# A planned two-layer decoder trunk on one core: the last norms by square root and reciprocal, fifteen weight loads taken from GpSimd, and six new seeds for the order

## The chip, the cores and the metric

The kernel runs on one core of a Trainium2 chip. The metric is the device time of one execution in microseconds (us), the median over several runs. The core has five engines that run side by side, each through its own list of instructions in a fixed order: TensorE (PE in the profile; PEld is its weight load), VectorE (DVE), ScalarE (ACT), GpSimd (POOL) and SyncE (SP, which here only issues transfers). Instructions of different engines wait for each other by semaphores. Transfers between the chip's memory and the on-chip buffers are done by DMA engines; SP issues most of them, GpSimd those that add what they read to what lies in the buffer.

## The reference

Two layers of a decoder over 512 positions and 1024 channels. Layer 0 mixes positions with a gated recurrence (RG-LRU), layer 1 with a chunked gated linear attention (GLA); each mixer is followed by a gated feed-forward net with a convolution of width 3. A condition vector `c` gives shift, scale and gate of each of the four sublayers.

```python
def rmsnorm(x, g):
    y = x32 * lax.rsqrt(jnp.mean(x32 * x32, axis=-1, keepdims=True) + EPS)
    return (y * g.astype(jnp.float32)).astype(x.dtype)

def reference(x, c, ada_w, ...):
    c_act = jax.nn.silu(c)
    for i in range(DEPTH):                                   # DEPTH = 2
        mod = (c_act @ ada_w[i] + ada_b[i])[:, None, :]
        sh_m, sc_m, gt_m, sh_f, sc_f, gt_f = jnp.split(mod, 6, axis=-1)
        h = rmsnorm(x, norm_g[i, 0]) * (1.0 + sc_m) + sh_m
        y = rglru_mixer(h, ...) if i % 2 == 0 else gla_mixer(h, ...)
        x = x + gt_m * rmsnorm(y, norm_g[i, 1])
        h = rmsnorm(x, norm_g[i, 2]) * (1.0 + sc_f) + sh_f
        y = conv_ffn(h, ffn_w_up[i], ffn_conv_w[i], ffn_conv_b[i], ffn_w_down[i])
        x = x + gt_f * rmsnorm(y, norm_g[i, 3])
    return x
```

## The kernel before

All matrix products are done in three passes of a reduced 32-bit format: each operand is split into a rounded part (hi) and a rest (lo), and TensorE sums hi·hi, hi·lo and lo·hi. So every weight that comes from memory (tile `raw`, mostly 128x1024, 512 KB) is prepared into two halves of a tile `w` (or into tiles `g`): ScalarE casts the first half (`CAST w<-raw`), and the second half, raw minus that cast, is made in one of two ways. In the first VectorE subtracts (`TENSOR_TENSOR w<-raw,w`). In the second, taken for the units that the rule `BYLOAD` picks, ScalarE writes the raw values rounded and negated (`ACTIVATE w<-raw`), and GpSimd issues a second transfer of the same 512 KB, which adds the weight from memory to that (`accum`), so that the rest is left. `load_upto` does this for one unit after another; units named `up` are columns of the feed-forward nets' first projection (layer, column), `gr` those of GLA's output gate, `gv` of its values, `rgg` of the recurrence's gate. GpSimd also issues 46 adding transfers that form sums of weight blocks for the down projections (tile `raw`); the change leaves these alone.

The stages in time are the prologue (norm of x, the condition's `adaT` products), RG-LRU, feed-forward 0, GLA (about 530 to 790 us), feed-forward 1 and `last_down` (from about 1085 us).

The order on each engine is not written by hand. The program first lists some thousand operations (`Sched.add`) with an estimated duration; `Sched.order` then simulates the engines and picks, whenever one is free, the ready operation of the highest priority. On TensorE and SP that is the place in the program. On VectorE, ScalarE and GpSimd it is the longest chain of work still behind the operation, plus a random nudge (`NUDGE` 0.5 us times a normal number, drawn from `SEEDS`, one seed for each of six segments of the program). Two limits bind the order to the buffers: `raw` and `araw` have 3 buffers each, `mm` 7 banks, `w` 8, so a transfer can be issued only when its buffer has been read for the last time.

`last_down` ends the kernel. For each of four tiles t of 128 positions TensorE makes 2 x 512 columns of the down projection into banks `mm`; VectorE adds each bank to y; ScalarE squares it and sums the squares (`Square` with an accumulator); `rstd_col` makes the norm's factor: `mean_of` on VectorE, then a power of -1/2 on GpSimd (`TENSOR_TENSOR sm<-sm,const`). VectorE multiplies y by the gate's rows, then adds factor times y to the residual `xo` (`SCALAR_TENSOR_TENSOR g<-const,sm,g`), which SP stores. For the last tile the second half is cut in two 256-wide parts, so that the chain after the last matmul is short, and its last 256 columns are scaled by ScalarE (`z`) and added by GpSimd. Between feed-forward 0 and GLA `gate_rows` writes a gate's 1024 values to memory and reads them back spread over all partitions (`g<-dram`).

Of the kernel before, what the change touches and what calls it, by code (L numbers as in the profile page):

```python
# [8 lines left out]
F32 = mybir.dt.float32  # L9
# [6 lines left out]
P = 128  # L16
# [258 lines left out]
BANK_AHEAD = 1  # L275
BANK_FROM = lambda s: s.mix2
LATE = 0.6, 0.6
SEEDS, NUDGE = (10, 10, 10, 10, 10, 10), 0.5
MARGIN = {"dve": 1.04, "act": 1.04}
RINGS = "araw",  # L280
ENGS = ("pe", "dve", "act", "pool", "sp")
# [364 lines left out]
                   after=after)  # L646


BYLOAD = lambda what, *i: what in ('rgg', 'gv', 'gr') or what == 'up' and (i[0] == 1 and i[1] >= KF and 4 <= i[1] - KF < 18 and i[1] % 2 or i[0] == 0 and i[1] >= KF and 4 <= i[1] - KF)
WARM = (3, 2, 2, 2)  # L650
KSPLIT = 2
NAH = 4
# [12 lines left out]
def trunk(ctx, tc, xT, x_d, wall, adaT, par_d, c_d, walpha_d, ident_d, masks_d, out):  # L665
# [363 lines left out]
    def rstd_col(ss, n):  # L1029
# [2 lines left out]
        e.pow(rp[0:1], mean_of(ss, n), nhalf[0:1])  # L1032
        return rp[0:1]

    xkept = {}

    def sublayer_out(sub, src, y, gate, nexth, held=None, xo=None, old=None):
# [75 lines left out]
    def last_down(hid, y, rows, xo, old):  # L1113

        for t in range(NT):
            old(t)
        for t in range(NT):
            last = t == NT - 1
            groups = [[(0, S)], [(S, S + 256)], [(S + 256, D)]] if last else [[(0, S), (S, D)]]
            ss = s.buf("sm", F32, 4)  # L1120
            yg = []
            i = 0
            for g in groups:
                for ps, (f0, f1) in zip(down_t("f1", hid, t, g), g):
                    yv = y[2 * t + f0 // S][f0 % S:f0 % S + f1 - f0]
                    e.tt(yv, yv, ps, ALU.add)
                    sq = gtn(f1 - f0)
                    e.act(sq, yv, AF.Square, accum=ss[i:i + 1])
                    i += 1
                    yg.append((yv, f0, f1))  # L1130
            rp = rstd_col(ss, i)
            for yv, f0, f1 in yg:
                e.tt(yv, yv, rows[f0 // S][f0 % S:f0 % S + f1 - f0], ALU.mult)
            ys = [y[2 * t + f][:] for f in range(2)]
            if last:

                z = gtn(256)
                e.act(z, ys[1].sub(256, S), AF.Copy, scale=rp)
                xr = xo[t, 1][256:S]
                e.tt(xr, xr, z, ALU.add, "pool")  # L1140
            for f, yv in enumerate(ys):
                for c0, c1 in ((0, 256), (256, S))[:2 - f] if last else ((0, S),):
                    xr = xo[t, f][c0:c1]
                    e.stt(xr, yv.sub(c0, c1), rp, xr, ALU.mult, ALU.add)
                e.store(out[t, :, f * S:(f + 1) * S], xo[t, f][:], P * S * 4)


    def conv3(layer, ps, m):
# [684 lines left out]
```

## Time and profile before

| | |
|---|---|
| runs, us | 1129.80, 1130.26, 1128.26; median 1129.80 |
| the profiled execution's own time | 1129.75 us |
| its span, first to last instruction | 1128.0 us |
| mean granted clock of TensorE | 0.997 |
| busy: TensorE, VectorE, ScalarE, GpSimd | 1105.5, 912.2, 673.9, 113.8 us |
| GpSimd's adding transfers | 95 (49 into `w`, 46 into `raw`) |

A row of the timeline reads: start, duration, engine, line, operation, output<-inputs, shapes, count; in brackets the time that the engine sat idle before it and what released it. A row of groups reads: line, engine, operation, names, shapes, count | busy us, mean ns of one | idle time before and its releasers. A row of windows reads: the stretch, its length, busy us of TensorE, weight load, VectorE, ScalarE, GpSimd with counts, then the granted clock, the DMA engines' busy share and GB/s. Buffer numbers are left out in all of them.

### The profile page before, as it was taken

Reading aid. Unit: us, or ns where it says so; the run is one execution under the profiler, and the core shown is the slowest. Engines: PE = TensorE matmul, PEld = TensorE weight load, DVE = VectorE, ACT = ScalarE, POOL = GpSimd, SP = SyncE. Lnnn points to the kernel's source line nnn. Section 1 sums busy time; section 2 is a strip of 40 time slices with the busy share of each in tenths; the row PEclk is TensorE's granted clock in tenths of the full one; section 3 lists DMA queues with packets and bytes.
Section 4 is the critical chain, followed back from the end, with each engine's and each line's share of the span. In section 5 each row is a group of like instructions: output and inputs, shape, how many; then the busy total and the mean of one; then the engine's idle time right before and its main releaser. Section 6 shows DMA issues by size and latency. Waiting matters only on the chain.

```text
span 1128.0 us, 14808 instructions
## 1 busy us (share of the span) xinstructions
PE 1105.5 (98%) x5293; PEld 919.2 (81%) x5293; DVE 912.2 (81%) x1559; ACT 673.9 (60%) x1039; POOL 113.8 (10%) x144
## 2 busy tenths in 40 slices
PE   7999999999999999999999999999999999999996
PEld 6776889888888888787888888889888888888885
DVE  6998999878878888898779797756876867777897
ACT  4569958656456354466797748656556454553432
POOL 0000011011101101101101101002000100010001
PEclk9999999999999999999999999999999999999998
DMA  9889876699898999873553927227487766767642
GB/s 362 287 249 294 285 235 241 168 260 315 240 267 243 273 269 263 204 221 116 151 141 107 302 78 206 94 100 241 112 257 211 198 188 157 199 158 196 169 130 75
DMA packets 67068, 232.97 MB, mean 207 GB/s; under 512 B 7473, under 2 KB 8145, under 8 KB 66994
## 3 DMA queue, kind: packets, MB, share of 16 engines
q1 hardware_dynamic: 53314, 182.73, 46.2%
q0 software_dynamic: 13680, 49.29, 24.0%
q8 instruction: 42, 0.69, 0.2%
q14 instruction: 32, 0.26, 0.1%
HBM read 225.68 MB, written 6.31 MB: 206 GB/s over the span
## 4 chain that ended last, share of the span: by engine, by line
PE 72%; DMA 14%; DVE 5%; ACT 4%; issue 3%; POOL 0%; SPq 0%; DVEq 0%; POOLq 0%; ACTq 0%
PE mm L621 71%; DMA raw<-in_wall_dram 10%; DMA w<-in_adaT_dram 2%; DVE w L544 1%; ACT g L594 1%; ACT w L601 1%; DMA g<-dram 1%; DVE g L544 1%; DVE g L558 1%; PE mm L628 1%; DMA const<-in_par_dram 1%; DVE const L544 1%; PE nr L621 1%; ACT w L594 0%; DVE const L558 0%
## 5 line engine op out<-in xcount | busy, mean ns | idle before, releaser
L621 PE MATMUL mm<-g,w 128*128 128x512 f32 (+2 forms) x2758 | 613.5, 380 | 1.1 <-DVE g L558 0.7
L621 PEld LDWEIGHTS mm<-g,w 128*128 128x128 f32 (+1 forms) x2758 | 501.0, 187 | 100.6 <-issue 1.4
L621 PE MATMUL mm<-w,g 128*128 128x512 f32 (+1 forms) x1428 | 330.6, 389 | 0.8 <-DVE g L544 0.8
L621 PEld LDWEIGHTS mm<-w,g 128*128 128x128 f32 x1428 | 265.2, 188 | 55.6 <-DVE g L544 1.2
L601 ACT CAST w<-raw 128x1024 fp32r<-128x1024 f32 x206 | 212.3, 1040 | 135.1 <-DMA raw<-in_wall_dram 122.0
L544 DVE TENSOR_TENSOR w<-raw,w 128x1024 fp32r<-128x1024 f32 x157 | 188.0, 1208 | 43.1 <-ACT w L601 42.8
L558 DVE SCALAR_TENSOR_TENSOR g<-mm,const,g 128x510 f32<-128x510 f32 (+3 forms) x199 | 147.9, 747 | 65.7 <-ACT g L594 62.7
L544 DVE TENSOR_TENSOR g<-g,g 128x256 f32<-128x256 f32 (+2 forms) x251 | 135.5, 564 | 32.6 <-ACT g L594 20.3
L594 ACT ACTIVATE g<-mm,const 128x512 f32<-128x512 f32 x115 | 86.6, 761 | 73.9 <-PE mm L621 73.1
L637 POOL DMA_DIRECT2D w<-in_wall_dram x49 | 42.6, 870 | 521.3 <-ACT w L594 417.1
L558 DVE SCALAR_TENSOR_TENSOR araw<-araw,const 128x1024 f32<-128x1024 f32 x72 | 86.7, 1219 | 5.9 <-DMA araw<-in_adaT_dram 5.9
L594 ACT ACTIVATE g<-g 128x512 f32<-128x512 f32 (+1 forms) x136 | 68.9, 541 | 26.1 <-DVE g L558 19.8
L601 ACT CAST g<-g 128x512 fp32r<-128x512 f32 (+2 forms) x84 | 49.9, 605 | 50.7 <-DVE g L544 50.7
L621 PE MATMUL mm<-g,g 128*128 128x256 f32 (+3 forms) x508 | 78.1, 309 | 1.1 <-DVE sm L569 1.1
L621 PEld LDWEIGHTS mm<-g,g 128*128 128x128 f32 (+1 forms) x508 | 70.5, 191 | 6.5 <-DVE g L544 1.3
L594 ACT ACTIVATE w<-raw 128x1024 fp32r<-128x1024 f32 x49 | 51.9, 1059 | 21.6 <-DMA raw<-in_wall_dram 20.0
L637 POOL DMA_DIRECT2D raw<-in_wall_dram x46 | 40.0, 869 | 198.3 <-ACT raw L594 47.2
L544 DVE TENSOR_TENSOR const<-const,mm 128x512 f32<-128x512 f32 (+1 forms) x81 | 53.4, 676 | 7.0 <-PE mm L621 6.6
L549 POOL TENSOR_TENSOR sm<-sm,const 128x1 f32<-128x1 f32 (+1 forms) x30 | 25.5, 854 | 271.5 <-DVE sm L558 237.7
L594 ACT ACTIVATE g<-const 128x512 f32<-128x512 f32 x47 | 29.0, 630 | 33.3 <-DVE const L544 19.6
L594 ACT ACTIVATE g<-mm 128x512 f32<-128x512 f32 x44 | 26.2, 596 | 27.6 <-DVE g L544 14.2
L594 ACT ACT_TABLE_LOAD x28 | 35.9, 1283 | 3.5 <-PE nr L621 2.3
(119 smaller groups left out, 752.8 us busy)
## 6 DMA issues: line engine op xcount, KB each, us to landing
raw<-in_wall_dram SPq DMA_DIRECT2D x218, 512.0 KB, 4.8
araw<-in_adaT_dram SPq DMA_DIRECT2D x72, 512.0 KB, 7.5
w<-in_wall_dram POOLq DMA_DIRECT2D x49, 512.0 KB, 8.4
raw<-in_wall_dram POOLq DMA_DIRECT2D x44, 512.0 KB, 8.1
w<-in_adaT_dram SPq DMA_DIRECT2D x24, 512.0 KB, 8.4
g<-dram SPq DMA_DIRECT2D x24, 256.0 KB, 5.7
dram<-const SPq DMA_DIRECT2D x8, 512.0 KB, 3.0
const<-in_xT_dram SPq DMA_DIRECT2D x4, 512.0 KB, 5.7
```

Source lines behind the costliest of these rows:

```text
L544: self.s.add(eng, dur, lambda: e.tensor_tensor(out.ap(), a.ap(), b.ap(), op=op), [a, b], [out])
L549: lambda: self.nc.gpsimd.tensor_tensor(out.ap(), a.ap(), b.ap(), op=ALU.pow), [a, b], [out])
L558: return self.nc.vector.scalar_tensor_tensor(out.ap(), a.ap(), f(sc), b.ap(), op0=op0, op1=op1, **kw)
L594: return self.nc.scalar.activation(out.ap(), a.ap(), func, **kw)
L601: self.s.add("act", (0.095 if self._sb(a) else 0.052) + out.n * 0.8325e-3, lambda: self.nc.scalar.copy(out.ap(), a.ap()), [a], [out], afte ...
L621: r.append(self.nc.tensor.matmul(g[0].ap(), g[1].ap(), g[2].ap(), start=g[3], stop=g[4], **kw))
L628: self.s.add("pe", 0.112, lambda: self.nc.tensor.transpose(out.ap(), a.ap(), ident.ap()), [a, ident], [out])
L637: self.s.add("pool", 0.9, lambda: self.nc.gpsimd.dma_start(out.ap(), src, accum_op=ALU.add), [out], [out], xfer=nbytes)
```

## The change

Four edits. `SEEDS` gets six other numbers, so that the three engines that are ordered by chains are planned anew. `BYLOAD` loses the eight `gr` units and the seven odd-numbered `up` units of layer 1: these 15 weights get their second half by VectorE's subtraction instead of by ScalarE's negation and GpSimd's transfer. In `last_down` the new `rstd_root` takes the place of `rstd_col`: ScalarE computes a square root with the mean of the earlier parts as its bias, and VectorE a reciprocal. And the last tile is finished like the others, by two 512-wide instructions of VectorE.

```diff
-SEEDS, NUDGE = (10, 10, 10, 10, 10, 10), 0.5
+SEEDS, NUDGE = (9127, 7551, 2985, 6212, 7264, 540), 0.5
...
-BYLOAD = lambda what, *i: what in ('rgg', 'gv', 'gr') or what == 'up' and (i[0] == 1 and i[1] >= KF and 4 <= i[1] - KF < 18 and i[1] % 2 or i[0] == 0 and i[1] >= KF and 4 <= i[1] - KF)
+BYLOAD = lambda what, *i: what in ('rgg', 'gv') or what == 'up' and i[0] == 0 and i[1] >= KF and 4 <= i[1] - KF
...
+    def rstd_root(ss, n):
+
+        rp = s.buf("sm", F32, 4)[0:1]
+        bias = mean_of(ss, n - 1) if n > 1 else epsc[0:1]
+        e.act(rp, ss[n - 1:n], AF.Sqrt, bias=bias, scale=1.0 / D, table=("sqrt",))
+        e.dve(0.13, lambda: nc.vector.reciprocal(rp.ap(), rp.ap()), [rp], [rp])
+        return rp
...
-            rp = rstd_col(ss, i)
+            rp = rstd_root(ss, i)
             for yv, f0, f1 in yg:
                 e.tt(yv, yv, rows[f0 // S][f0 % S:f0 % S + f1 - f0], ALU.mult)
-            ys = [y[2 * t + f][:] for f in range(2)]
-            if last:
-
-                z = gtn(256)
-                e.act(z, ys[1].sub(256, S), AF.Copy, scale=rp)
-                xr = xo[t, 1][256:S]
-                e.tt(xr, xr, z, ALU.add, "pool")
-            for f, yv in enumerate(ys):
-                for c0, c1 in ((0, 256), (256, S))[:2 - f] if last else ((0, S),):
-                    xr = xo[t, f][c0:c1]
-                    e.stt(xr, yv.sub(c0, c1), rp, xr, ALU.mult, ALU.add)
-                e.store(out[t, :, f * S:(f + 1) * S], xo[t, f][:], P * S * 4)
+            for f in range(2):
+                xr = xo[t, f][:]
+                e.stt(xr, y[2 * t + f][:], rp, xr, ALU.mult, ALU.add)
+                e.store(out[t, :, f * S:(f + 1) * S], xr, P * S * 4)
```

The number of instructions in the order goes from 1447 to 1460 on VectorE, from 956 to 950 on ScalarE and from 146 to 126 on GpSimd; it stays at 371 on SP, and TensorE's order is the same but for buffer numbers. The places that the prediction speaks of follow; numbers behind names are those of buffers, and they differ between the two kernels for the same thing.

VectorE at the end of the program, before: `mm` is the last bank, `const_8` is y, `g_1696` and `g_1697` are the gate's rows, `sm_1964` is GpSimd's factor of the last tile, and `g_1933`, `g_1934` are the last tile's residual halves.

```order
L544 TENSOR_TENSOR const_8_98<-const_8_98,mm_1960_10069 128x256
L558 SCALAR_TENSOR_TENSOR g_1932_9907<-const_8_98,sm_1956_10049,g_1932_9907 128x512
L558 SCALAR_TENSOR_TENSOR sm_1961_10078<-sm_1958_10063,sm_1961_10078 128x1
L544 TENSOR_TENSOR const_8_98<-const_8_98,g_1697_8539 128x256
L558 SCALAR_TENSOR_TENSOR g_1934_9915<-const_8_98,sm_1964_10098,g_1934_9915 128x256
L558 SCALAR_TENSOR_TENSOR g_1933_9909<-const_8_98,sm_1964_10098,g_1933_9909 128x256 x2
```

The same engine and place now:

```order
L544 TENSOR_TENSOR const_8_98<-const_8_98,mm_1960_10052 128x256
L569 TENSOR_SCALAR sm_1962_10073<-sm_1958_10046 128x1
L544 TENSOR_TENSOR const_8_98<-const_8_98,g_1697_8528 128x256
L558 SCALAR_TENSOR_TENSOR sm_1962_10073<-sm_1958_10046,sm_1962_10073 128x1
L558 SCALAR_TENSOR_TENSOR g_1925_9867<-const_8_98,sm_1943_9957,g_1925_9867 128x512
L1040 RECIPROCAL sm_1964_10080<-sm_1964_10080 128x1
L544 TENSOR_TENSOR const_8_98<-const_8_98,g_1697_8528 128x256
L558 SCALAR_TENSOR_TENSOR g_1933_9894<-const_8_98,sm_1964_10080,g_1933_9894 128x512
L558 SCALAR_TENSOR_TENSOR g_1934_9900<-const_8_98,sm_1964_10080,g_1934_9900 128x512
```

The mean of the first parts now stands before the last square is needed, a reciprocal has come in, a 512-wide addition of tile 0 (`g_1925`) has been left until here, and two 512-wide additions stand where three 256-wide ones stood.

GpSimd at the end of the program, before: one transfer, the four powers (one for each tile) and the addition of the last quarter.

```order
L637 DMA raw_1867_9520<-in_wall_dram 128x512
L549 TENSOR_TENSOR sm_1943_9970<-sm_1942_9962,const_4_90 128x1
L549 TENSOR_TENSOR sm_1950_10002<-sm_1949_9994,const_4_90 128x1
L549 TENSOR_TENSOR sm_1956_10049<-sm_1955_10040,const_4_90 128x1
L549 TENSOR_TENSOR sm_1964_10098<-sm_1961_10078,const_4_90 128x1
L544 TENSOR_TENSOR g_1934_9915<-g_1934_9915,gh_1965_10101 128x256
```

The same engine and place now:

```order
L637 DMA raw_1804_9141<-in_wall_dram 128x1024
L637 DMA raw_1816_9221<-in_wall_dram 128x1024
L637 DMA raw_1819_9233<-in_wall_dram 128x1024
L637 DMA raw_1841_9355<-in_wall_dram 128x1024
L637 DMA raw_1863_9474<-in_wall_dram 128x1024
L637 DMA raw_1865_9496<-in_wall_dram 128x512
```

GpSimd's last instruction is now a transfer for the down projection, with no arithmetic behind it.

SP between feed-forward 0 and GLA, before: the two loads of the gate's rows (`g_917`, `g_918`, read back from `dram_905`) stand ahead of the next weight (`raw_919`).

```order
L632 DMA g_910_4589<-dram_391_1757 128x512
L632 DMA g_912_4593<-dram_391_1757 128x512
L632 DMA g_917_4611<-dram_905_4569 128x512
L632 DMA g_918_4613<-dram_905_4569 128x512
L632 DMA raw_919_4620<-in_wall_dram 128x1024
```

The same place now:

```order
L632 DMA g_911_4589<-dram_392_1762 128x512
L632 DMA g_913_4593<-dram_392_1762 128x512
L632 DMA raw_916_4601<-in_wall_dram 128x1024
L632 DMA g_918_4612<-dram_906_4569 128x512
L632 DMA g_919_4614<-dram_906_4569 128x512
```

The weight has moved ahead of the gate's two rows.

VectorE in feed-forward 0, at about 468 us of the profile, before: two products of the second condition layer (`araw`) stand behind the convolution (`128x510`) and ahead of the addition that empties the bank `mm_840`.

```order
L558 SCALAR_TENSOR_TENSOR g_835_4174<-mm_822_4116,const_9_103,g_835_4174 128x510
L558 SCALAR_TENSOR_TENSOR araw_805_4015,const_522_2473<-araw_805_4015,const_23_131 128x1024
L544 TENSOR_TENSOR const_568_2712<-const_568_2712,const_9_103 128x8
L558 SCALAR_TENSOR_TENSOR araw_784_3895,const_522_2473<-araw_784_3895,const_23_131 128x1024
L544 TENSOR_TENSOR g_492_2327<-g_492_2327,mm_840_4211 128x512
```

The same place now:

```order
L558 SCALAR_TENSOR_TENSOR g_836_4182<-mm_822_4113,const_9_103,g_836_4182 128x511
L558 SCALAR_TENSOR_TENSOR g_836_4182<-mm_822_4113,const_9_103,g_836_4182 128x510
L558 SCALAR_TENSOR_TENSOR araw_800_3998,const_518_2449<-araw_800_3998,const_23_131 128x1024
L544 TENSOR_TENSOR g_493_2331<-g_493_2331,mm_838_4203 128x512
L544 TENSOR_TENSOR g_498_2351<-g_498_2351,mm_841_4211 128x512
```

One of the two products has gone from this place.

VectorE in the prologue, at about 30 us, before: `w_61` is a product with a row of the first layer's condition matrix, `g_76` the rest of a slice of the normed input, for which TensorE waits.

```order
L569 TENSOR_SCALAR const_72_319<-const_9_103 128x8
L544 TENSOR_TENSOR const_73_321<-const_9_103,const_71_317 128x8
L569 TENSOR_SCALAR const_71_317<-const_71_317 128x8
L558 SCALAR_TENSOR_TENSOR w_61_245,const_42_179<-w_61_245,const_23_131 128x1024
L558 SCALAR_TENSOR_TENSOR g_76_339<-g_67_299,const_44_186,g_75_330 128x512
```

The same place now:

```order
L569 TENSOR_SCALAR const_72_319<-const_9_103 128x8
L544 TENSOR_TENSOR const_73_321<-const_9_103,const_71_314 128x8
L569 TENSOR_SCALAR const_71_314<-const_71_314 128x8
L558 SCALAR_TENSOR_TENSOR g_76_335<-g_67_299,const_44_186,g_75_330 128x512
L558 SCALAR_TENSOR_TENSOR w_60_243,const_42_179<-w_60_243,const_23_131 128x1024
```

The two have changed places.

## Prediction

> **What bounds the kernel now.** I read the page's busy shares first, then TensorE's waits, then windows, then the timeline of the end. The page gives each engine's busy time:
>
> ```profile
> PE 1105.5 (98%) x5293; PEld 919.2 (81%) x5293; DVE 912.2 (81%) x1559; ACT 673.9 (60%) x1039; POOL 113.8 (10%) x144
> ```
>
> TensorE is busy for all but 22.5 of 1128.0 us, and its order does not change. So the change can gain only where TensorE sits idle, and lose only by making it idle. Its waits, grouped by what ended them (total, times, longest):
>
> ```profile
> PE nr L621 <- DVE gh L544: 3.5, 1, 3.5
> PE mm L621 <- DMA araw<-in_c_dram: 2.4, 1, 2.4
> PE mm L628 <- ACT gh L594: 2.0, 3, 1.1
> PE mm L628 <- ACT g L594: 1.5, 4, 0.6
> PE mm L621 <- DVE sm L569: 1.1, 1, 1.1
> ```
>
> The first two are the prologue's, which the change does not touch. The others are short and scattered. What is left is the stretch behind the last matmul, some 9.9 us. Windows over GLA, over feed-forward 1 and over the last stage:
>
> ```profile
> 580.00:720.00 140.00, 140.00 (x775) 120.04 (x774) 118.47 (x243) 100.25 (x184) 11.98 (x15) 1.00 0.52 150
> 790.00:1060.00 270.00, 270.00 (x1204) 223.91 (x1203) 202.73 (x300) 139.31 (x182) 24.19 (x28) 1.00 0.70 184
> 1100.00:1120.00 20.00, 18.09 (x92) 15.28 (x90) 18.79 (x39) 5.96 (x18) 3.23 (x4) 1.00 0.18 66
> ```
>
> In the first two TensorE never stops, and VectorE has 21.5 and 67.3 us free. The end, in order of time:
>
> ```profile
> 1116.73 1.36 PE L621 MATMUL mm<-w,g 128*128 128x256 f32 x10
> 1118.13 0.42 DVE L544 TENSOR_TENSOR const<-const,mm 128x256 f32<-128x256 f32 x1
> 1118.47 0.75 DVE L558 SCALAR_TENSOR_TENSOR g<-const,sm,g 128x512 f32<-128x512 f32 x1
> 1118.58 0.42 ACT L594 ACTIVATE gh<-const 128x256 f32<-128x256 f32 x1 [0.93 <-DVE const L544]
> 1119.13 0.16 DVE L558 SCALAR_TENSOR_TENSOR sm<-sm,sm 128x1 f32<-128x1 f32 x1
> 1119.20 0.42 DVE L544 TENSOR_TENSOR const<-const,g 128x256 f32<-128x256 f32 x1
> 1119.43 0.59 POOL L549 TENSOR_TENSOR sm<-sm,const 128x1 f32<-128x1 f32 x1 [3.81 <-DVE sm L558]
> 1120.06 1.74 DVE L558 SCALAR_TENSOR_TENSOR g<-const,sm,g 128x256 f32<-128x256 f32 x3 [0.43 <-POOL sm L549]
> 1120.64 0.88 POOL L544 TENSOR_TENSOR g<-g,gh 128x256 f32<-128x256 f32 x1 [0.62 <-ACT gh L594]
> ```
>
> Arithmetic is over at 1121.80, 6.2 us before the end of the span. Behind it stand the last store and the closing instructions, whose rows give durations (min, median, max, ns) and the first and last start; a third row gives stores from issue to landing:
>
> ```profile
> L1828 POOLq DRAIN  x3: 40/93/6600, 1120.6 to 1127.7; - x3
> L1828 SPq DRAIN  x3: 7/7/7, 1124.7 to 1127.5; - x3
> DMA to landing us min/median/max: 2.1/2.3/2.5
> ```
>
> The last store, issued at about 1122.2, lands at 1124.5, and SP's closing drain starts at 1124.7. GpSimd's is the long one: it starts at 1120.6, when its addition has been handed over, and takes 6.6 us, to 1127.2. All engines meet behind it, and 0.8 us later the span ends. So the end waits 2.5 us for GpSimd alone.
>
> **The tail.** In the new order GpSimd's last work is a transfer in feed-forward 1, tens of microseconds earlier; its drain should then run and end there, under TensorE's matmuls. I walk the new end with the durations above, from the same last matmul. The last bank is added until 1118.55, and ScalarE's square with its reading of the sum ends by 1119.1. The square root is new: the nearest row is an activation on 128x1 with a scale and a bias that are tiles,
>
> ```profile
> L594 ACT ACTIVATE const<-const,const,const 128x1 f32<-128x1 f32 x8 | 3.1, 386 | 10.2 <-DVE w L558 10.2
> L594 ACT ACT_TABLE_LOAD x28 | 35.9, 1283 | 3.5 <-PE nr L621 2.3
> ```
>
> 0.39 us, so 1119.5. Meanwhile VectorE multiplies by the gate (0.42), finishes the mean of the first parts (0.16) and does tile 0's late 512-wide addition (0.75), to about 1119.7: this, not the root, ends last. The reciprocal on 128x1 I price like VectorE's small instructions, 0.16 us; nothing excludes twice that. Then 0.42 for the gate's other part, its start overlapping, to 1120.15, and two additions of 0.75 with starts some 0.67 apart, to 1121.5. The three 256-wide ones before took 1.74 us, more than two of 0.75, since the last ran beside GpSimd's addition. The last store is issued at 1121.53, lands 2.3 later at 1123.8, SP needs 0.2 and the common close 0.8: 1124.8 against 1128.0, a gain of 3.2 us. Of it 2.5 is GpSimd's drain and 0.7 the shorter chain. One more table load precedes tile 0's root; it is 1.28 us by the row, and ScalarE has 14 of 20 us free there.
>
> Here a rule weighs against me. The Trainium skill, "VectorE: DVE Perf Modes", section "The DRAIN you can't avoid", says that the drains at a kernel's start and close take some 12 ns on every engine. The trace disagrees for GpSimd, with 6600 ns against SP's 7. If the rule holds all the same, those 6.6 us are no cost of GpSimd's own but a wait for the end, and only the 0.7 us come: that is the first rival below.
>
> **The fifteen weights.** Each loses a negation and an adding transfer, and gains a subtraction:
>
> ```profile
> L544 DVE TENSOR_TENSOR w<-raw,w 128x1024 fp32r<-128x1024 f32 x157 | 188.0, 1208 | 43.1 <-ACT w L601 42.8
> L594 ACT ACTIVATE w<-raw 128x1024 fp32r<-128x1024 f32 x49 | 51.9, 1059 | 21.6 <-DMA raw<-in_wall_dram 20.0
> L637 POOL DMA_DIRECT2D w<-in_wall_dram x49 | 42.6, 870 | 521.3 <-ACT w L594 417.1
> ```
>
> VectorE gets 15 x 1.208 = 18.1 us more, ScalarE 15.9 and GpSimd 13.1 us less, and 7.9 MB less is moved. Eight subtractions (9.7 us) fall in GLA, where VectorE has 21.5 us free; seven (8.5 us) in feed-forward 1, with 67.3 free. None of the three engines holds TensorE in these windows, so the saving is worth nothing and the cost is covered by that idle time. If the cover is gone, a subtraction delays what stands behind it on VectorE by up to 1.21 us each; its `raw` buffer is also held until then, so SP's next weight would be late next. I charge 0.4 us, one third of one subtraction; the bounds are 0 and all eight of GLA, 9.7 us, which is a rival. The nearest row, TensorE's 140.00 of 140, puts it near 0.
>
> **The order.** New seeds change VectorE, ScalarE and GpSimd, and through buffers SP. Four places matter. In the prologue:
>
> ```profile
> 29.63 1.22 DVE L558 SCALAR_TENSOR_TENSOR w<-w,const 128x1024 f32<-128x1024 f32 x1 [1.18 <-DMA w<-in_adaT_dram]
> 30.78 0.75 DVE L558 SCALAR_TENSOR_TENSOR g<-g,const,g 128x512 fp32r<-128x512 f32 x1
> 31.58 1.66 PE L621 MATMUL mm<-g,w 128*128 128x512 f32 x6 [0.74 <-DVE g L558]
> ```
>
> VectorE waited for a condition row and worked on it while TensorE's operand stood behind. Now the operand goes first, so the whole 0.74 should go. In feed-forward 0:
>
> ```profile
> 469.25 1.22 DVE L558 SCALAR_TENSOR_TENSOR araw<-araw,const 128x1024 f32<-128x1024 f32 x1
> 470.39 1.28 DVE L544 TENSOR_TENSOR g<-g,mm 128x512 f32<-128x512 f32 x2
> 471.13 1.66 PE L621 MATMUL mm<-w,g 128*128 128x512 f32 x6 [0.79 <-DVE g L544]
> ```
>
> TensorE waited for the bank which the first of the two additions empties. With one product fewer ahead the addition comes 1.2 us earlier: 0.79 gained. At the turn into GLA's other half:
>
> ```profile
> 778.54 1.06 ACT L594 ACTIVATE raw<-raw 128x1024 f32<-128x1024 f32 x1 [0.41 <-DMA raw<-in_wall_dram]
> 779.50 1.91 ACT L594 ACTIVATE gh<-mm,const 128x256 f32<-128x256 f32 x4
> 780.56 0.66 PE L628 MATMUL mm<-const,g 128*128 128x128 f32 x4 [1.08 <-ACT gh L594]
> ```
>
> ScalarE's reading of banks stood behind the negation of a weight that came late, because VectorE freed its buffer late; that subtraction now stands earlier. TensorE's other two waits for `gh` share 2.0 - 1.08, about 0.46 each, which seems to be the floor, so 0.6 is gained (between 0 and 1.08).
>
> Against this stands the transition to GLA:
>
> ```profile
> 20.00:40.00 20.00, 19.25 (x97) 16.18 (x98) 17.65 (x30) 9.37 (x16) 1.64 (x1) 1.00 1.00 377
> 520.36 0.69 DVE L544 TENSOR_TENSOR const<-const,g 128x512 f32<-128x512 f32 x1 [1.54 <-DMA g<-dram]
> 528.38 0.66 PE L628 MATMUL mm<-const,g 128*128 128x128 f32 x4 [0.35 <-ACT g L594]
> ```
>
> VectorE waits 1.54 us for the gate's rows, and SP now issues a 512 KB weight ahead of them. At the 377 GB/s of the window in which the DMA engines were full that is 1.4 us. TensorE's wait at 528.38 would grow by that at most; but other VectorE work has moved ahead into the gap, and the 1.1 us wait for `sm` later in the same chain can absorb some. I take 0.5 lost, between 0.3 gained and 1.5 lost.
>
> **The sum.** 1129.75 - 3.2 - 0.74 - 0.79 - 0.6 + 0.5 + 0.4 = 1125.3 us. It is made on the profiled execution, 0.05 under the median of 1129.8 and 1.75 over its span; I keep both offsets. The three runs differ by 2.0 us; about 0.2%, 2.3 us, is what a measurement tells from no change: faster means under 1127.5, slower over 1132.1.
>
> **Rivals.** First, the drain stays at the end: GpSimd's 6.6 us are bound to the close, and the tail gains 0.7. For it: the other engines' drains take nanoseconds, and no row shows GpSimd's drain earlier in a busy program. Against: it starts at 1120.6 when its own queue is empty, not when SP's is, and ends 2.5 us after SP has finished. 1127.8.
>
> Second, the order costs elsewhere: the weight ahead of the gate's rows costs its full 1.4, 0.9 more than I charge, and of the three small gains, 2.1 together, half is lost to what is late next at those places. 1125.3 + 0.9 + 1.1 = 1127.3; against no change that is within what can be told. For it: gains at single places were read off an order, and what comes up behind them can only be walked, not seen.
>
> Third, slower: VectorE becomes the bound in GLA. Its free 21.5 us there are partly waits for ScalarE's results; if they cannot be filled, each of the eight subtractions makes TensorE late: 1125.3 - 0.4 + 9.7 = 1134.6. The kernel is slower than before from the sixth of the eight on (1124.9 + 6 x 1.21 = 1132.2). For it: VectorE is 85% busy there. Against: TensorE does not wait once in 140 us, so VectorE runs well ahead.
>
> **The numbers.** The forecast has 0.65, the drain 0.16, the order 0.12, VectorE's bound 0.07. The forecast lies wholly under 1127.5; of the drain and the order a little over a third does: 0.65 + 0.10 = 0.75 faster, 0.18 same, 0.07 slower. The predicted time is 1125.3. With the transition, the stray 0.4, the wait at 780.56 and the store's landing at their good ends (0.8, 0.4, 0.5 and 0.2) it would be 1123.4, and a run can lie some 0.4 lower; the first two rivals reach 1.0 over 1127.8 in the same way: range 1123.0 to 1128.8.
>
> **What would show it.** Right: the last matmul near 1116 us and the span ending some 6.7 us behind it instead of 9.9; GpSimd's long drain starting well before the last matmul; TensorE without its waits at 31.6 and 471.1, and under 1.9 us at 528; some 930 us busy on VectorE, 80 adding transfers. Wrong: a drain of GpSimd that ends last; idle TensorE between 580 and 720; a wait for a `raw` transfer there.

## The result and the profile after

The changed kernel took 1125.08 us in the median of seven runs (1123.03 to 1127.41), against 1129.80 of seven runs of the kernel before: a ratio of 0.9962, 95% interval 0.9946 to 0.9978. Twelve later runs, beside 29 of the kernel before, gave 1127.67 against 1128.65, 0.9983 (0.9967 to 0.9998). Both intervals lie under 1, so the changed kernel is faster, but by how much is less sure. The forecast was 1125.3 us, a gain of some 4.5. The first set's gain, 4.3 us (2.5 to 6.1), holds that; the second set's, 1.9 us (0.2 to 3.7), does not, and it is less than the 2.3 us that the prediction asked for before it would say faster. The changed kernel's runs spread wider than those of before (1122.4 to 1131.4 us in the later set, against 1127.2 to 1133.3).

The profiled execution took 1127.41 us, the slowest of the first seven, with a span of 1125.6. A second profile of the same kernel, from the later set, took 1124.01 with a span of 1122.2. It is shown beside the first because the two differ where it matters. The first page's busy times:

```profile
PE 1106.1 (98%) x5293; PEld 920.1 (82%) x5293; DVE 924.6 (82%) x1573; ACT 660.0 (59%) x1028; POOL 96.0 (9%) x124
```

VectorE does 12.4 us more, ScalarE 13.9 and GpSimd 17.8 less than before, where 18.1, 15.9 and 13.1 were worked out for the fifteen weights alone and the end's edits move some work too; TensorE is busy 0.6 us more. The end, by rows of the first profile's timeline:

```profile
1099.66 19.58 PE L621 MATMUL mm<-w,g 128*128 128x512 f32 x97
1119.27 0.42 DVE L544 TENSOR_TENSOR const<-const,mm 128x256 f32<-128x256 f32 x1
1119.73 0.42 ACT L594 ACTIVATE gh<-const 128x256 f32<-128x256 f32 x1 [0.44 <-DVE const L544]
1120.08 0.74 DVE L558 SCALAR_TENSOR_TENSOR g<-const,sm,g 128x512 f32<-128x512 f32 x1
1120.27 0.29 ACT L594 ACTIVATE sm<-sm,sm 128x1 f32<-128x1 f32 x1
1120.74 0.16 DVE L1040 RECIPROCAL sm<-sm 128x1 f32<-128x1 f32 x1
1120.81 0.41 DVE L544 TENSOR_TENSOR const<-const,g 128x256 f32<-128x256 f32 x1
1121.13 1.41 DVE L558 SCALAR_TENSOR_TENSOR g<-const,sm,g 128x512 f32<-128x512 f32 x2
```

The last matmul ends at 1119.24 and arithmetic 3.3 us later, at 1122.54; before, it was 3.7 us. As walked, tile 0's late addition, not the root, holds the reciprocal. The closing instructions (durations min, median, max in ns, first and last start), and the stores from issue to landing:

```profile
L1828 POOLq DRAIN  x3: 40/102/9205, 1051.2 to 1125.3; - x3
L1828 SPq DRAIN  x3: 7/7/7, 1124.7 to 1125.0; - x3
DMA to landing us min/median/max: 2.0/2.0/2.1
```

GpSimd's long drain now starts at 1051.2, right at its last transfer, takes 9.2 us and has ended 59 us before the last matmul does. Nothing waits for it. From the last matmul's end to the end of the span it is 6.36 us instead of 9.91.

So the end gained 3.55 us, but the span only 2.4: in this execution the last matmul itself came 1.15 us later than before. TensorE's waits:

```profile
PE nr L621 <- DVE gh L544: 2.9, 1, 2.9
PE mm L621 <- DMA w<-in_wall_dram: 2.3, 1, 2.3
...
PE mm L628 <- ACT gh L594: 1.7, 3, 0.8
PE mm L621 <- ACT g L594: 1.1, 1, 1.1
```

and its timeline where it sat idle, of the first profile; then rows of the second profile's timeline, the last of them its last matmuls:

```profile
16.76 0.71 PE L621 MATMUL mm<-const,sm 128*128 128x128 f32 x4 [0.74 <-POOL sm L549]
99.50 5.78 PE L621 MATMUL mm<-g,w 128*128 128x512 f32 x24 [1.10 <-ACT g L594]
464.12 6.92 PE L621 MATMUL mm<-g,w 128*128 128x512 f32 x22 [2.28 <-DMA w<-in_wall_dram]
```

```profile
99.60 5.73 PE L621 MATMUL mm<-g,w 128*128 128x512 f32 x24 [0.15 <-ACT g L594]
470.95 1.67 PE L621 MATMUL mm<-w,g 128*128 128x512 f32 x6 [0.42 <-DVE g L544]
1100.79 15.05 PE L621 MATMUL mm<-w,g 128*128 128x512 f32 x77
```

The waits at 31.58, 528.38 and 748 us of before are gone, but three new ones stand in the first profile, the largest at 464 us on a weight that GpSimd's transfer brings late. In the second profile, the same program, that wait is absent, the last matmul ends at 1115.84, 2.25 us earlier than before, and the end stretch is again 6.36 us.

The wait at 464 us cost more than its 2.28 us. These are windows over the place, of the first profile and of the second; the third number from the end is the granted clock:

```profile
455.00:477.00 22.00, 19.72 (x81) 15.79 (x80) 17.04 (x28) 10.68 (x14) 4.34 (x5) 0.92 0.85 206
455.00:477.00 22.00, 21.58 (x95) 17.53 (x94) 16.98 (x26) 9.42 (x12) 2.77 (x4) 1.00 0.89 222
```

In the first profile the granted clock fell behind the wait, and the 22 matmuls that follow it took 6.92 us. In e11 below, with a wait of 2.27 us at the same place and a granted clock of 1.00, the same 22 matmuls took 5.28 us. So about 1.6 us of this execution went to the lower clock, and a wait of this length does not always bring it.

Between 580 and 720, and from 790 to 1060 us, VectorE's added work has cost nothing (first profile):

```profile
580.00:720.00 140.00, 140.00 (x774) 120.16 (x773) 126.63 (x252) 93.65 (x180) 5.03 (x7) 1.00 0.41 124
790.00:1060.00 270.00, 270.00 (x1209) 224.21 (x1208) 210.23 (x307) 134.45 (x178) 18.15 (x21) 1.00 0.64 171
```

VectorE is busy 8.2 and 7.5 us more there, and TensorE still does not wait once.

### The profile page after: what moved, and what is told of

The parts are those of the page before. It is cut to its first block, busy times and chain, and to the rows that moved or that the text cites. A ratio compares the mean times of both kernels' runs of the same rounds, so it can differ in the third digit from the quotient of the medians.

```text
span 1125.6 us, 14788 instructions
## 1 busy us (share of the span) xinstructions
PE 1106.1 (98%) x5293; PEld 920.1 (82%) x5293; DVE 924.6 (82%) x1573; ACT 660.0 (59%) x1028; POOL 96.0 (9%) x124
## 3 DMA queue, kind: packets, MB, share of 16 engines
HBM read 217.82 MB, written 6.31 MB: 199 GB/s over the span
## 4 chain that ended last, share of the span: by engine, by line
PE 64%; DMA 12%; DVE 9%; issue 7%; ACT 6%; POOL 1%; DVEq 0%; SPq 0%; POOLq 0%; ACTq 0%
PE mm L621 63%; DMA raw<-in_wall_dram 10%; ACT g L594 3%; DVE g L558 3%; DVE w L544 2%; ACT w L601 2%; DVE w L558 1%; DVE g L544 1%; DMA w<-in_adaT_dram 1%; DMA w<-in_wall_dram 1%; DVE araw L558 1%; ACT L594 1%; PE mm L628 1%; DVE const L544 1%; ACT w L594 1%
## 5 line engine op out<-in xcount | busy, mean ns | idle before, releaser
L544 DVE TENSOR_TENSOR w<-raw,w 128x1024 fp32r<-128x1024 f32 x172 | 205.6, 1208 | 53.5 <-ACT w L601 51.2
L544 DVE TENSOR_TENSOR g<-g,g 128x256 f32<-128x256 f32 (+3 forms) x251 | 134.7, 563 | 21.1 <-ACT g L594 11.4
L637 POOL DMA_DIRECT2D w<-in_wall_dram x34 | 29.7, 873 | 353.9 <-ACT w L594 236.3
L594 ACT ACTIVATE w<-raw 128x1024 fp32r<-128x1024 f32 x34 | 36.0, 1058 | 13.9 <-DMA raw<-in_wall_dram 13.9
L549 POOL TENSOR_TENSOR sm<-sm,const 128x1 f32<-128x1 f32 (+1 forms) x26 | 21.7, 834 | 229.2 <-DVE sm L558 205.2
```

The lines of the kernel that those rows point to most:

```text
L544: self.s.add(eng, dur, lambda: e.tensor_tensor(out.ap(), a.ap(), b.ap(), op=op), [a, b], [out])
L549: lambda: self.nc.gpsimd.tensor_tensor(out.ap(), a.ap(), b.ap(), op=ALU.pow), [a, b], [out])
L594: return self.nc.scalar.activation(out.ap(), a.ap(), func, **kw)
L637: self.s.add("pool", 0.9, lambda: self.nc.gpsimd.dma_start(out.ap(), src, accum_op=ALU.add), [out], [out], xfer=nbytes)
```

## The experiments

Each kernel was timed against the kernel before unless said otherwise. "End stretch" is the time from the end of the last matmul (last row of TensorE's timeline) to the end of the span. "Matmul at 550 us" is the start of one matmul of GLA, the same in all kernels.

| kernel | ratio to before (95%) | matmul at 550 us | last matmul ends | span | end stretch |
|---|---|---|---|---|---|
| before | 1 | 549.26 | 1118.09 | 1128.0 | 9.91 |
| changed, first profile | 0.9962 (0.9946 to 0.9978) | 551.48 | 1119.24 | 1125.6 | 6.36 |
| changed, second profile (e13) | 0.9983 (0.9967 to 0.9998) | 547.79 | 1115.84 | 1122.2 | 6.36 |
| e1, end alone | 0.9976 (0.9964 to 0.9987) | 552.25 | 1121.38 | 1128.0 | 6.62 |
| e2, seeds alone | 1.0011 (0.9995 to 1.0026) | 550.25 | 1118.85 | 1129.4 | 10.55 |
| e3, weights alone | 0.9985 (0.9973 to 0.9997) | 548.58 | 1116.39 | 1125.2 | 8.81 |
| e4, GpSimd work beside the root | 0.9980 (0.9963 to 0.9997) | 550.30 | 1118.44 | 1125.3 | 6.86 |
| e5, the same 5 us earlier, on the third tile | one run, 1125.03 us | 548.50 | 1116.76 | 1123.2 | 6.44 |
| e8, the same behind everything | one run, 1132.99 us | 554.45 | 1122.21 | 1131.1 | 8.89 |
| e6, 18 more weights by VectorE | 1.0059 (1.0038 to 1.0080) | 548.90 | 1126.12 | 1132.7 | 6.58 |
| e9, changed with old seeds | 0.9973 (0.9959 to 0.9987) | 547.50 | 1115.49 | 1122.7 | 7.21 |
| e10, changed with old third seed | 1.0042 (1.0025 to 1.0058) | 559.24 | 1127.09 | 1133.4 | 6.31 |
| e11, changed with 95 transfers | 0.9999 (0.9982 to 1.0016) | 551.99 | 1119.87 | 1127.8 | 7.93 |
| e12, e9 with earlier tiles finished first | 0.9975 (0.9964 to 0.9987) | 550.81 | 1118.68 | 1125.7 | 7.02 |

From the matmul at 550 us to the end of the last one it is 568.8 us in the kernel before, 569.1 in e1 and 568.6 in e2; in the changed kernel and all others but e6 it is 567.8 to 568.3, and in e6 577.2. So most of what sets one profile's last matmul apart from another's lies ahead of 550 us. And there many of these kernels are alike. On every engine e1, e3, e9 and e12 run the same instructions in the same order as the kernel before until about 590 us; e2, e4, e5, e8 and e11 run those of the changed kernel as far. Yet the matmul starts anywhere from 547.50 to 552.25 us in the five profiles with the old seeds, and from 547.79 to 554.45 in the seven with the new ones. That is what executions of one order differ by.

**e1, the end alone.** The kernel before with `rstd_root` and with the last tile's two 512-wide additions, as in the change.

> The kernel before with the end of the changed one alone (square root and reciprocal, last tile by VectorE), old seeds, old 95 adding transfers. Drain theory (GpSimd's closing drain runs its own time from GpSimd's last arithmetic, 2.5 us past SP's close, and the new end takes that arithmetic away): the stretch from the last matmul's end to the end of the span shrinks from 9.9 to between 6.3 and 6.7 us, the drain starts before the last matmul, and the time falls by 3.2 to 3.6 us, about 0.3%. Close theory (the long drain waits for the end of the program, whatever GpSimd does): the stretch shrinks by 0.7 us at most and the drain still ends last. No new wait of TensorE by either, since the orders are those of before but for the last stage.

The closing drain of GpSimd in this kernel:

```profile
L1828 POOLq DRAIN  x3: 40/93/10886, 1056.5 to 1127.8; - x3
```

It starts at 1056.5 and the end stretch is 6.62, inside the 6.3 to 6.7 of the drain theory. The time fell by 0.24%, 2.7 us (1.5 to 4.1). Not as expected: TensorE did wait anew, 1.63 us at 473 and 0.44 at 468, in orders that are those of before up to the last stage. The place between 455 and 477 us is one where executions of the same order differ.

**e4, e5 and e8, one GpSimd instruction put back.** The changed kernel with a 128x1 addition on GpSimd that nobody reads, whose input is ready beside the last root (e4), on the third tile (e5) or behind the last addition (e8).

```diff
+            if last:                                   # e4; in e5: if t == 2
+                e.tt(s.buf("sm", F32, 4)[0:1], ss[i - 1:i], ss[i - 1:i], ALU.add, "pool")
...
+                if last and f:                         # e8, behind the last stt
+                    e.tt(s.buf("sm", F32, 4)[0:1], xr.sub(0, 1), xr.sub(0, 1), ALU.add, "pool")
```

> The changed kernel with one GpSimd instruction more, a 128x1 addition of the last tile's sum of squares whose result nobody reads; it starts at about 1120.3 us of the changed kernel's profile, beside the square root. Drain theory: GpSimd's drain starts then, lasts 6 us or more, ends at about 1126.5, and the span ends 0.8 later: the end stretch grows from 6.35 to about 8 us or more, time 1.5 to 2.5 us above the changed kernel. Close theory: the end stretch stays at 6.35 us within 0.2. Chain theory (the gain of the end came from the shorter chain of norm and last additions): likewise no growth.

> The changed kernel with the same added GpSimd instruction as in the run with the late one, but on the third tile's sum of squares, about 5 us earlier. Drain theory: GpSimd's drain starts about 1115, ends 4.5 to 5.7 us behind the instruction, about 1120 to 1121, well before SP's close, and the end stretch is 6.35 us within 0.2. A theory in which any late GpSimd work costs time (a port, a queue) expects 6.8 us or more, as with the late one.

> The changed kernel with one 128x1 addition on GpSimd that reads the last result of the kernel, so that it ends about 0.5 us behind VectorE's last instruction; nobody reads it. Drain theory: GpSimd's drain ends 4.5 to 5.7 us behind that addition, so some 4 us behind SP's close; the stretch from the last matmul to the end of the span grows from 6.35 us to between 9 and 10.5. Close theory: it stays at 6.35 within 0.3.

The addition and the closing drains of GpSimd and SP, for e5, e4 and e8 in this order:

```profile
1112.75 0.54 POOL L544 TENSOR_TENSOR sm<-sm 128x1 f32<-128x1 f32 x1 [62.85 <-ACT g L594]
L1830 POOLq DRAIN  x3: 40/102/5038, 1112.7 to 1122.9; - x3
L1830 SPq DRAIN  x3: 7/7/7, 1122.4 to 1122.7; - x3
```

```profile
1119.64 0.43 POOL L544 TENSOR_TENSOR sm<-sm 128x1 f32<-128x1 f32 x1 [68.22 <-ACT gh L594]
L1830 POOLq DRAIN  x3: 40/93/4923, 1119.6 to 1125.0; - x3
L1830 SPq DRAIN  x3: 7/7/7, 1123.9 to 1124.8; - x3
```

```profile
1125.70 0.19 POOL L544 TENSOR_TENSOR sm<-g 128x1 f32<-128x1 f32 x1 [70.33 <-DVE g L558]
L1830 POOLq DRAIN  x3: 40/102/4682, 1125.7 to 1130.9; - x3
L1830 SPq DRAIN  x3: 7/7/7, 1127.7 to 1130.6; - x3
```

The long drain is the maximum in each row, and it begins at the first start: 1112.7 + 5.04 = 1117.7, 1119.6 + 4.92 = 1124.5, 1125.7 + 4.68 = 1130.4. It follows GpSimd's last instruction, ending about 4.5 us behind its end each time, and is not tied to the close. Where it ends before SP's drain (e5) it costs nothing, 6.44 us against 6.36; where it ends 0.6 us behind (e4) the stretch is 0.5 longer; 2.6 us behind (e8), 2.5 longer. The drain theory holds, and the close theory and the theory that only the shorter chain counted fall. The sizes were put too high (8 and 9 to 10.5 us expected, 6.86 and 8.89 measured), because the drain takes 4.5 us here and not 5.7 as in the kernel before. That is not the smaller addition's doing: e3, below, ends with the 256-wide addition of before and has 4.5 as well.

**e2, the seeds alone.** The kernel before with the change's `SEEDS`.

> The kernel before with the six new seeds alone. Place theory (the order gains what was read off at 31.6, 471 and 780 us and loses at the transition to GLA): TensorE's waits at 31.6 and 471.1 gone, the end of the last matmul 1 to 2 us earlier, the end stretch unchanged at 9.9 us, time 1 to 2 us lower. Shuffle theory (a new order removes some short waits and brings others of the same size): TensorE's idle time between 12 us and the last matmul stays within 2 us of before, at other places, and the time is the same within 0.2%.

TensorE's timeline, two of the places that are new:

```profile
99.70 5.74 PE L621 MATMUL mm<-g,w 128*128 128x512 f32 x24 [0.86 <-ACT g L594]
462.84 5.32 PE L621 MATMUL mm<-g,w 128*128 128x512 f32 x22 [1.43 <-DMA w<-in_wall_dram]
```

The waits at 31.58, 528.38 and 748 are gone and these have come; the wait at 471 stayed (0.72 at 473). From 12 to 1115 us TensorE is idle for 6.9 us, against 6.6 before. The last matmul ends 0.76 us later than before, the end stretch is 0.6 longer, and the time is not to be told from no change. The shuffle theory holds, the place theory falls.

**e3, the weights alone.** The kernel before with the change's `BYLOAD`.

> The kernel before with the 15 weights' second halves by VectorE alone, old seeds, old end. Cover theory: TensorE stays without a wait from 580 to 720 us, VectorE is busy 9 to 10 us more there and 8 us more from 790 to 1060, the end stretch stays at 9.9 us, and the time is within 2 us of before. Bound theory (VectorE ends last in GLA): TensorE idles several us between 560 and 740, and the time rises by up to 9.7 us. Transfer theory (the adding transfers were what made raw transfers and weights late): TensorE's idle time falls by 1 us or more with no help from the seeds.

TensorE stays busy for 140 of 140 us in GLA with VectorE at 126.27, so the bound theory falls. The time fell by 0.15%, 1.7 us, and the waits at 528, 748 and 780 shrank or went. But the wait at 528 lies ahead of the first instruction that this edit moves, at about 590 us, so its going is chance; and e2 lost the wait at 748 with all 95 transfers in place. Behind the matmul at 550 us e3 is 1.0 us shorter than before. Another 1.1 us come from where none were expected, the end stretch, which was to stay at 9.9 us and is 8.81. GpSimd's last addition, the same as in the kernel before, and its drains:

```profile
1118.94 1.01 POOL L544 TENSOR_TENSOR g<-g,gh 128x256 f32<-128x256 f32 x1 [0.62 <-ACT gh L594]
L1828 POOLq DRAIN  x3: 40/93/5512, 1118.9 to 1124.9; - x3
```

The long drain ends at 1118.9 + 5.51 = 1124.4, about 4.5 us behind the addition's end at 1119.95, where it was 5.7 in the kernel before and in e2. Those two kernels issue 95 adding transfers on GpSimd, and e3, e4, e5 and e8 issue 80; whether their number sets the drain was not tried by itself. The new end takes the drain off the path anyway, so this part of e3's gain and the gain of e1 cannot be added.

**e11, the changed kernel with the 95 transfers.** The edit of e3 backwards, in the changed kernel.

> The changed kernel with the old 95 adding transfers (new seeds, new end). Load theory (taking 15 weights off GpSimd is worth about 1.7 us by itself, as in the run of that part alone, whatever the order): 1.5 to 3 us above the changed kernel, and one or more of TensorE's waits behind ScalarE or a weight's transfer come back. Order theory (the 1.7 us of that run came from the plan that happened to follow, not from the loads): within 1 us of the changed kernel.

It came out even with before, and 1.8 us above the second set of the changed kernel in ratio (0.9999 against 0.9983, with overlapping intervals). The load theory would take that as its gain. The profile does not let it: the end stretch is 7.93 us in this plan, 1.6 more than in the changed kernel, with GpSimd's drain long over (it starts at 1053.8), so most of the difference can lie in how VectorE's last instructions were ordered. From the matmul at 550 us to the end of the last one it is 567.88 us here, against 567.76 and 568.05 in the changed kernel's two profiles: with these seeds the fifteen adding transfers cost TensorE nothing that shows. With the old seeds (e3) taking them away came with 1.0 us there. What the weights themselves are worth in time stays open, nothing included.

**e9 and e10, other seeds.** The changed kernel with `(10, 10, 10, 10, 10, 10)`, and with `(9127, 7551, 10, 6212, 7264, 540)`.

> The changed kernel with the six old seeds. Sum theory (the parts add up: end -2.7, weights -1.7 us by the two single runs, seeds +1.2): 1125.2 us or lower, equal to the changed kernel or up to 1.2 us faster; last matmul at about 1116.4 us as in the run of the weights alone, end stretch 6.35 us, span about 1122.8 in a run without late weights at 460 us. Joint-plan theory (the new seeds were worth something only together with the other edits): 1 us or more above the changed kernel.

> The changed kernel with the old seed in the third of six segments alone (second half of feed-forward 0), the others new. Order theory: TensorE's waits at 460 to 475 us fall from 2.3 us to under 1, and the last matmul comes 1 to 3.5 us earlier, time 1 to 2.5 us under the changed kernel. Chance theory (weights are late there in some executions of any order, as in the run of the end alone): the place loses between 0.5 and 4 us as before, time within 1 us of the changed kernel.

With the old seeds the kernel is as fast as the changed one, within the intervals; its profile has the 1122.7 us span that was expected, and the last matmul at 1115.49 instead of 1116.4, but an end stretch of 7.21 instead of 6.35. Its median, 1126.25 us, is above the 1125.2 of the sum theory, and the intervals do not decide between the two theories. With one seed of six exchanged the kernel is 0.42% slower than before. The wait that seed was to remove is still there, and another has come at 524 us:

```profile
PE mm L621 <- ACT g L601: 4.1, 1, 4.1
...
PE mm L621 <- DMA w<-in_wall_dram: 2.3, 1, 2.3
```

All that e10 loses lies ahead of 550 us: its matmul there starts at 559.24, and from there on it is as fast as the changed kernel. Part of the loss is again the clock, granted at 0.91 from 520 to 560 us. So the order theory of e10 falls, and the chance theory with it, as to the time: the old seed, which goes with a fast kernel in e9, goes with a slow one here, among other seeds.

**e6, no adding transfers for feed-forward weights.**

```diff
+BYLOAD = lambda what, *i: what in ('rgg', 'gv')
```

> The changed kernel with the other 18 adding transfers of feed-forward weights (layer 0) taken off GpSimd too, as the change did with those of layer 1: 62 adding transfers instead of 80, 18 more subtractions on VectorE (18 x 1.21 = 21.7 us between 200 and 530 us). Adding-transfer theory (the new wait of 2.3 us at 464 us is one such weight, negated late and landed 9 us after its issue, and without the second trip it is ready about 5 us sooner): that wait goes, no other of its size comes, and the time is 1.5 to 3 us under the changed kernel. VectorE theory (feed-forward 0 has no room for 21.7 us more): several waits on VectorE between 200 and 530 us, time 2 us or more above the changed kernel. Order theory (the third seed's order makes raw weights late between 455 and 475 us, by whichever way they are split): a wait of 1 us or more for a raw weight stays there.

The wait at 464 us went, as the adding-transfer theory says. That does not show the second trip to be its cause, since the wait is absent also in e5 and in the changed kernel's second profile, where that weight makes its second trip. The time rose to 0.6% above before, by waits on VectorE, and not where they were expected: between 200 and 530 us TensorE is busy for all of 330.00. They stand in GLA (waits from 530 to 745 us):

```profile
PE mm L621 <- DVE g L544: 4.1, 4, 1.4
PE mm L621 <- DVE g L558: 3.4, 2, 2.5
PE mm L1010 <- DVE g L558: 1.6, 1, 1.6
```

That is some 9 us of waiting for VectorE in GLA, one step beyond the change, and looks like the third rival. But VectorE is busy for 188 of these 215 us, and the whole order behind 205 us is a new one: whether VectorE has no room for the work or the order places it badly stays open.

**e12, earlier tiles finished first.** e9 with the stores of tiles 0 to 2 counted four times as large in the plan.

```diff
-                e.store(out[t, :, f * S:(f + 1) * S], xr, P * S * 4)
+                e.store(out[t, :, f * S:(f + 1) * S], xr, P * S * 4 * (1 if last else 4))
```

> The changed kernel with old seeds, and in the plan alone the stores of the first three tiles counted four times as large, so that VectorE finishes those tiles before the last tile's chain: behind the last bank's addition it has only the gate's products, the reciprocal and the last two additions. Same work, same orders up to the last stage. Queue theory (left-over additions of earlier tiles stand in the last chain on VectorE; in the old-seed run three of them, 2.1 us): the end stretch falls from 7.2 us in that run to between 5.9 and 6.4, the time is 0.8 to 1.3 us under that run's. Rival (VectorE, busy 93% in the last 20 us, delays a bank instead, and TensorE waits): end stretch shorter, but the last matmul later by as much.

Missed: 7.02 us instead of 5.9 to 6.4, and the time like e9's. The left-over additions are out of the chain, but the last tile's mean now comes late on VectorE, and the root waits for it:

```profile
1120.72 0.29 ACT L594 ACTIVATE sm<-sm,sm 128x1 f32<-128x1 f32 x1 [0.43 <-DVE sm L558]
```

No version was found that is clearly faster than the changed kernel.

**e13, the changed kernel again.**

> The changed kernel once more, for comparison on the same chip and at the same time. Late-weight theory (the weights between 455 and 475 us come late by an amount that differs from execution to execution): the wait for a weight at 464 us is there again with another size, and the loss between 455 and 475 us against the kernel before, 3.1 us in the profile shown, lies anywhere between 1 and 4. By a fixed order alone it would repeat within 0.3.

The late-weight theory is right that the place differs from execution to execution, and went not far enough: the wait at 464 us was to come again, and it is absent. A loss that repeats within 0.3 us, as by a fixed order alone, is out. The two executions of the same program, first profile and second, at the negation of that weight and its adding transfer:

```profile
453.64 1.06 ACT L594 ACTIVATE w<-raw 128x1024 fp32r<-128x1024 f32 x1 [0.57 <-DMA raw<-in_wall_dram]
454.99 0.86 POOL L637 DMA_DIRECT2D w<-in_wall_dram  x1 [12.28 <-ACT w L594]
```

```profile
450.47 1.06 ACT L594 ACTIVATE w<-raw 128x1024 fp32r<-128x1024 f32 x1 [0.76 <-DMA raw<-in_wall_dram]
451.82 0.86 POOL L637 DMA_DIRECT2D w<-in_wall_dram  x1 [12.87 <-ACT w L594]
```

The weight's first trip ended 3.2 us earlier in the second, though TensorE was only 0.4 us further there. It had been issued earlier; the first start in each row is SP's issue of this weight, again of the first profile and of the second:

```profile
449.08 12.57 SPq L632 DMA_DIRECT2D raw<-in_wall_dram  x5
444.67 18.53 SPq L632 DMA_DIRECT2D raw<-in_wall_dram  x6
```

From there to the negation it is 4.6 and 5.8 us, so the trip was no longer in the execution that lost time. SP was late. The two executions issue the same transfer 0.5 us apart at 229 us, 2.3 apart at 344 and 3.7 apart at 424. So the delay grew over some 200 us in which TensorE did not wait, and the wait at 464 us is where it came out. Why SP's transfers fall behind in one execution and not in the other is not settled.

## Why the prediction was right

**The tail, right in size and in cause.** Forecast 3.2 us, of which 2.5 from the drain and 0.7 from the shorter chain; the end stretch fell by 3.55 in both profiles, by 3.3 in e1, and the time of e1 by 2.7 (1.5 to 4.1). e4, e5 and e8 show the cause. From SP's first closing drain to the end of the span it is about 2.5 us less than before, and from the last matmul to that drain about 1.1 less, not 0.7: arithmetic ended 3.3 us behind the last matmul instead of the walk's 3.4, and the last store landed in 2.0 instead of 2.3. The root took 0.29 us instead of 0.39, which is worth nothing, as VectorE's late addition ended after it. The rule of the Trainium skill ("VectorE: DVE Perf Modes", section "The DRAIN you can't avoid") that such drains take some 12 ns holds for SP's 7 and not for GpSimd's 4.7 to 11.0 us; the rival built on it is out.

**The fifteen weights, right that they are covered.** 140.00 of 140 and 270.00 of 270 again. The 0.4 us charged for strays was of the wrong kind: the new waits are single ones (0.74, 1.10, 2.28 us) and stand ahead of 590 us, where the first of these weights is made.

**The order, wrong place by place.** The sum of its terms was a gain of 1.2 us with the 0.4 charged; the last matmul came 1.15 later in one profile and 2.25 earlier in the other, so the sum fell between them by luck. The step that failed is to read four waits off one execution, to price them as the order's, and to take the rest as unchanged. Executions of the old order differ by more than all four terms together. This is the first of the four places in e1, e3 and e9, whose orders there are those of before:

```profile
31.70 4.83 PE L621 MATMUL mm<-g,w 128*128 128x512 f32 x20 [0.17 <-DVE g L558]
31.43 4.83 PE L621 MATMUL mm<-g,w 128*128 128x512 f32 x20 [1.24 <-DVE g L558]
31.61 4.83 PE L621 MATMUL mm<-g,w 128*128 128x512 f32 x20 [1.76 <-DVE g L558]
```

The wait goes from 0.17 to 1.76 us, and the matmuls start at nearly the same time all the same, 31.58 in the kernel before: the wait tells how early TensorE came, not what there was to gain. At 471 us TensorE waited 1.63 us in e1, 0.81 in e3 and not at all in e9; the wait at 528 was 0.84 in e1 and absent in e3, e9 and e12. What the new seeds are worth ahead of 550 us cannot be told from such profiles; behind it the changed kernel is 0.8 and 1.1 us shorter than before.

Place by place, in the changed kernel: the 0.74 at 31.58 came in the first profile, and went again by 106 us, where ScalarE's work stands in another order (the wait at 99.50); in the second a wait of 0.96 for ScalarE stood at 30.43 instead. The 0.79 at 471 came in the first profile and in half in the second (0.42 left), and stood behind a new wait at 464. At 780 the longest wait for `gh` went from 1.08 to 0.8 and 1.0, not to 0.46. The transition to GLA was to cost 0.5 and gained: in the second profile, whose matmuls from 495 to 522 us start within 0.02 us of the same ones of before, VectorE starts on the gate's rows at the old time, although the weight goes ahead of them.

```profile
520.19 0.69 DVE L544 TENSOR_TENSOR const<-const,g 128x512 f32<-128x512 f32 x1 [0.21 <-DMA g<-dram]
```

Before it was 520.36 after 1.54 us of idling. So 512 KB ahead cost those rows nothing; the 1.4 us worked out from the full rate had no ground, perhaps because the weight that followed the rows before had shared the engines with them. VectorE meanwhile had filled the gap, and the wait at 528 went, as it did in three of the five profiles with the old order.

**The rivals.** The drain at the end is refuted. One argument for it was misread: that the other engines' drains take nanoseconds holds for SP alone. In the kernel before, the first closing drains of TensorE, VectorE and ScalarE took 2.35, 1.78 and 0.54 us, each until the engine's own last instruction ended. The order that costs elsewhere is nearer to e2, with 1.2 us lost (from 0.6 gained to 2.9 lost) where 1.6 were to be gained: it had the mechanism, at 12 in 100, and should have had more. VectorE as the bound did not come; e6 has waits for VectorE one step beyond the change.

## What to carry to other kernels

GpSimd's last work sets when its closing drain can run: let GpSimd finish early, or count its drain behind its last instruction, and look for the end of the drain against that of the last store. Where a planner with random nudges sets the order, a new seed moves short waits from place to place; a gain read off one place is not a gain of the sum, and here one seed of six cost 0.6 to 0.8%. And when one kernel's runs differ by several us, profile it twice before explaining or pricing a wait: here the largest new one was in one execution and not in the next, and waits of one and the same order went from 0.17 to 1.76 us. Kernels whose orders agree up to a point serve as repeated profiles up to there.

## What the runs showed of the hardware

GpSimd's first closing drain took 4.5 to 5.7 us from the end of its last arithmetic instruction (4.5 in e3, e4, e5 and e8, which issue 80 adding transfers, 5.7 in before and e2, which issue 95), and 8.3 to 10.1 us from the end of its last transfer's issue (8.3 in the first profile of the changed kernel, 10.1 in e11). In the kernel before, those of TensorE, VectorE and ScalarE ended within 0.1 us of the engine's own last instruction.

Behind a wait of TensorE of 2.28 us (changed kernel, first profile) and one of 2.98 us (e8) at the same place the granted clock fell to 0.92 in the window from 455 to 477 us; behind waits of 2.27 us (e11) and 1.75 us (e4) there it stayed at 1.00.

A switch of ScalarE's function table cost 1.30 us on ScalarE, from the load's start to the start of the next activation:

```profile
1107.40 1.28 ACT L594 ACT_TABLE_LOAD   x1 [1.79 <-DVE sm L569]
1108.70 0.29 ACT L594 ACTIVATE sm<-sm,sm 128x1 f32<-128x1 f32 x1
```
